# Index dot products of two query tiles in another order, selection rounds paced two and then three a unit, and one scaling moved from VectorE to ScalarE

## The chip, the cores and the metric

One core of a Trainium2 chip runs the whole kernel. The metric is device time in microseconds (us), the median of several executions. TensorE (PE, with its weight loads PEld) multiplies, VectorE (DVE), ScalarE (ACT) and GpSimd (POOL) work on vectors, SyncE (SP) issues most DMAs. Each engine runs its instructions in the order in which they were put into its queue.

## The reference

One decoder layer on 512 tokens and 16 prepended meta tokens (528 positions, width 1024): half-step SwiGLU FFN, a mixer, half-step SwiGLU FFN. The mixer has four heads of differential attention ("kind 0") and four heads of indexer-selected sparse attention ("kind 1"). For the second kind an indexer scores every key for every query, and only the top 128 keys of a query are attended to:

```python
u = rmsnorm(h, mix_norm) @ w_in
qa, ka, va, qb, ckv, iq, ik, iw = split(u)
# per block of 128 queries
dots = einsum('bqhd,bkd->bqhk', iq, ik)                  # 8 index heads of 64
score = einsum('bqh,bqhk->bqk', iw * 8 ** -0.5, relu(dots * 64 ** -0.5))
_, sel = top_k(where(causal, score, -inf), min(128, stop))
q_lat = rmsnorm(einsum('blhd,hdc->blhc', qb, b_w_uk))    # 4 heads, 256 wide
s = einsum('bqhc,bqkc->bhqk', q_lat, c[sel]) * 256 ** -0.5 + bias
```

## The kernel before

The program is one straight line of instructions without loops at run time. FFN 1 and FFN 2 (roughly the first 350 us and the last 340 us) are not touched. Matrix products are made in two parts, high and low: ACT writes the rounded high part, DVE subtracts to get the low part, and TensorE does three products (high by high, high by low, low by high).

The mixer has two stages.

**Projection stage** (about 380 to 475 us). A key projection `ik` and four index query projections `iq0` to `iq3` (line 1040, 24 matmuls of 512 columns each; `iq` c holds index heads 2c and 2c+1) come first, then three projections by `natural` (line 916). `pe_q` (line 873) is a list of small pieces of work, one per query tile t and index head hd: `dots_unit(t, hd)` (line 942) does two matmuls (line 949), a ReLU on ACT (line 951) and a multiply-add into the score of the tile on DVE (lines 954 and 957). `fill(1)` takes one piece off the list: `iq2` and `iq3` call it after each of their eight weight chunks, `natural` after each tile and half (12 matmuls). Tiles 0 to 3 have 144, 272, 400 and 528 keys. After the last head of tile 0 a small step drops its lowest keys (line 977). After the last head of tile 1, sixteen selection rounds and a mask go into DVE's queue at lower priority (line 962). A round (line 988) finds the eight largest scores and strikes them out, two passes over the tile's scores. For tiles 2 and 3 sixteen rounds and a mask each are appended to the list `selects` instead: 34 entries, used later.

**Attention stage** (about 475 to 670 us). 32 units, in the order of line 1139: kind 0 heads 0, 1, 2, kind 1 head 0, kind 0 head 3, kind 1 heads 1, 2, 3, each with query tiles 0 to 3. So units 0 to 11 are of kind 0, units 12 to 15 are the first of kind 1, and 16 to 19 are of kind 0 again. Step i of the loop (line 1465) holds the softmax of unit i (`u_soft`, line 1244, whose bias-add and minimum on DVE is line 1253), the normalisation of unit i-1, transposes and splits of unit i-2, `select(3)`, and the scores of unit i+1. `select(k)` (line 1238) takes k entries off `selects` and puts them behind the DVE work of the step, at slightly lower priority. A unit of kind 1 and tile t adds the mask of its tile on POOL (`u_mask`, line 1208, called one step ahead), so tile 2's mask is needed by unit 14 and tile 3's by unit 15. Other projections run as filler between units. `q_latent(hd)` (line 1373) makes the query of a kind 1 head in pieces, one per step: three products per tile, evacuation with a scale on ACT (line 1383), sums of squares on ACT (line 1389), a reciprocal root, four multiplications of a 128x256 tile by a column on DVE (line 1394), then transposes (line 1399) and their split (lines 1401, 1402).

The order on each engine is not the order of the text alone: a scheduler places instructions by priority when it expects their inputs, so a piece may slide past others.

Of the kernel before, what the change touches and what calls it, by code (L numbers as in the profile page):

```python
# [14 lines left out]
AF = mybir.ActivationFunctionType  # L15
# [38 lines left out]
def f32(ap):  # L54
    return ap.bitcast(F32)
# [145 lines left out]
def layer(ctx: ExitStack, tc: tile.TileContext, xT, gcols, kvg, lamv, rel, onehot,  # L201
# [4 lines left out]
    PE, V, A, G = nc.tensor, nc.vector, nc.scalar, nc.gpsimd  # L206
# [12 lines left out]
    def pa(name):  # L219
        return cur[0].tile([P, 2, 512], F32, tag="pa", bufs=3, name=name)  # L220
# [79 lines left out]
    def rsqrt_start(o, ss, n):  # L300

        A.activation(o, ss, AF.Ln, scale=1.0 / n, bias=epst)
        A.activation(o, o, AF.Exp, scale=-0.5)
# [576 lines left out]
    def proj_t(ps, full, nfill=0, w=None):  # L880
        wh, wl = w or ws.get()
        wh = wh[:, :1024].rearrange("p (k m) -> p k m", k=KC)
        wl = wl[:, :1024].rearrange("p (k m) -> p k m", k=KC)
        cols = [(0, T // 2), (T // 2, T)] if full else [(META, T)]
        for k in range(KC):
            for p_, (w, x) in enumerate(((wh, hgh), (wh, hgl), (wl, hgh))):
                for i, (a, b) in enumerate(cols):
                    o = ps[:, i, : b - a] if full else ps[:, : b - a]
                    PE.matmul(o, w[:, k, :], x[:, k, a:b], start=(k == 0 and p_ == 0),  # L889
                              stop=(k == KC - 1 and p_ == 2))  # L890
            if nfill and k % nfill == nfill - 1:
                fill(1)
# [49 lines left out]
    def dots_unit(t, hd):  # L942
        c, b = hd // 2, 64 * (hd % 2)
        K = kts(t)
        parts = [(0, K)] if K <= 512 else [(0, K // 2), (K // 2, K)]
        for (u0, u1) in parts:
            ps = dot_bank()[:, : u1 - u0]
            for p_, r in enumerate((ikh, ikl)):
                PE.matmul(ps, (iqh, iql)[hd % 2][c][:, t * P: (t + 1) * P], r[:, u0:u1], start=(p_ == 0), stop=(p_ == 1))
            rl = tmp[hd % 2][:, u0:u1]  # L950
            A.activation(rl, ps, AF.Relu, scale=I_D ** -0.5)
            sc = scores[t][:, u0:u1]
            if hd == 0:
                V.scalar_tensor_tensor(sc, rl, wq[:, t, hd: hd + 1], bias_win(cau, t)[:, u0:u1],
                                       op0=OP.mult, op1=OP.add if t == 0 else OP.subtract)
            else:
                V.scalar_tensor_tensor(sc, rl, wq[:, t, hd: hd + 1], sc, op0=OP.mult, op1=OP.add)
        if hd == I_H - 1 and t >= 2:
            selects.extend([lambda: topk_round(t)] * (TOPK // 8))
            selects.append(lambda: topk_mask(t))  # L960
        elif hd == I_H - 1:
            with tc.high_priority(offset=-1000):
                if t == 0:
                    drop_lowest()
                else:
                    for r in range(TOPK // 8):
                        topk_round(t)
                    topk_mask(t)
# [47 lines left out]
    def queue_dots(ts, hds):  # L1016
        for t in ts:
            for hd in hds:
                pe_q.append(lambda t=t, hd=hd: dots_unit(t, hd))
# [20 lines left out]
    for c in range(4):  # L1040
        ps = pa(f"iq{c}")[:, 0, :]
        proj_t(ps, False, 1 if c > 1 else 0)

        for q, r, o in ((iqh[c], 0, 64), (iql[c], 64, 0)):
            A.activation(q[r: r + 64], ps[r: r + 64], AF.Copy)
            V.tensor_sub(q[o: o + 64], ps[r: r + 64], f32(q[r: r + 64]))
        if c == 1:
            queue_dots((0, 1), range(4))
    queue_dots((0, 1), range(4, 8))
    queue_dots((2, 3), range(8))  # L1050

    def ckv_finish():
# [79 lines left out]
    def bank(tag):  # L1132
        return pp2.tile([P, 512], F32, tag=tag, bufs=nbank[tag], name=f"p_{tag}")
# [104 lines left out]
    def select(k):  # L1238

        with tc.issue_after(last[0].ins), tc.high_priority(offset=-100):  # L1240
            for _ in range(min(k, len(selects))):
                selects.pop(0)()
# [130 lines left out]
    def q_latent(hd):  # L1373
        ukh, ukl = uku
        qlraw = buf["ql"][:, :1024].rearrange("p (t c) -> p t c", t=NQ)
        ss = small.tile([P, NQ], F32, tag="qss", name="qss")
        for t in range(NQ):
            if t % 2 == 0:
                pq = bank("ch").rearrange("p (b c) -> p b c", b=2)
            for p_, (l, r) in enumerate(((qbh, ukh), (qbh, ukl), (qbl, ukh))):  # L1380
                PE.matmul(pq[:, t % 2, :], l[hd][:, t * P: (t + 1) * P], r[:, hd, :],
                          start=(p_ == 0), stop=(p_ == 2))
            A.activation(qlraw[:, t, :], pq[:, t % 2, :], AF.Copy, scale=Rn[:, t + 1: t + 2])
        qdone.add(hd)
        yield
        y = small.tile([P, NQ], F32, tag="rqy", bufs=2, name="rqy")
        w = small.tile([P, NQ], F32, tag="rqw", bufs=2, name="rqw")
        for t in range(NQ):
            A.activation(qll[hd][:, 0, :DC], qlraw[:, t, :], AF.Square, accum_out=ss[:, t: t + 1])
        rsqrt_start(y, ss, DC)  # L1390
        yield
        rsqrt_refine(y, ss, DC, w)
        for t in range(NQ):
            V.tensor_scalar_mul(qlraw[:, t, :], qlraw[:, t, :], y[:, t: t + 1])
        yield
        for c in range(2):
            pt = bank("ch")
            for t in range(NQ):
                PE.transpose(pt[:, t * P: (t + 1) * P], qlraw[:, t, c * P: (c + 1) * P], ident)
            g = gb[:, c: c + 1]  # L1400
            A.activation(qlh[hd][:, c, :], pt, AF.Copy, scale=g)
            V.scalar_tensor_tensor(qll[hd][:, c, :], pt, g, f32(qlh[hd][:, c, :]),
                                   op0=OP.mult, op1=OP.subtract)
            if c == 0:
                yield
        qready.add(hd)
# [39 lines left out]
    def advance(gs_, k=99):  # L1446
        for g in list(gs_)[:k]:
            if next(g, 1) == 1:
                gs_.remove(g)
# [14 lines left out]
    i = 0  # L1464
    while i < n or chains or qchains or st:
        if 0 <= i - 1 < n:
            u_norm(i - 1)
        advance(chains)
        if 0 <= i - 2 < n:
            u_trans(i - 2)  # L1470
        if i < n:
            u_soft(i)
        advance(qchains, 1)
        if 0 <= i - 2 < n:
            u_high(i - 2)
        advance(chains)
        if 0 <= i - 2 < n:
            u_low(i - 2)
        select(3)
        if i + 1 < n:  # L1480
            u_mask(i + 1)
            score_step(i + 1)
        if 0 <= i - 2 < n and units[i - 2][2] == NQ - 1:
            kind, hd, t = units[i - 2]
            b = bsel[(i - 2) // 4]
            G.tensor_copy(aM[b][32: 32 + META, :], f32(aM[b][:META, :]))
            chains.append((head_a, head_b)[kind](hd, b))
            next(chains[-1])
        if i == QS:
            fill_to(99)  # L1490
            uku += [w[:, :1024].rearrange("p (h c) -> p h c", h=B_H) for w in ws.get(ahead=False)]
            for x in ("ql", "vv", "sq"):
                buf[x] = wpool.tile([P, WSLOT], F32, tag="raw", bufs=3, name=f"buf_{x}")
            wo_load(0)
            stage += [buf["sq"][:, x * SEQ: (x + 1) * SEQ] for x in range(2)]
            late_load(0)
            late_conv(0)
        if QS < i <= QS + 6:
            x = i - QS - 1
            if x % 2 == 0:  # L1500
                q_b(1 + x // 2, lw)
            else:
                late_conv((x + 1) // 2)
            if x == 5:
                uvu += [w[:, :1024].rearrange("p (h c d) -> p h c d", h=B_H, c=2) for w in lw]
                clear(aM[1])
        for hd in range(A_H):
            if i == max(QS + 2 * hd, units.index((0, hd, NQ - 1))):
                qchains.append(q_latent(hd))
        fill_to(fill_at[i] if i < len(fill_at) else 99)  # L1510
        if all(h in adone for h in range(KA)):
            ready += 0.8
        while wo_done <= KC and (wo_done < int(ready) or i == n - 1):
            wo_step(wo_done)
            wo_done += 1
        if i == n - 1:
            ws.limit = n_plain2
            ws.conv(V)
        i += 1
# [109 lines left out]
```

## Time and profile before

| | us |
|---|---|
| median of 3 runs | 1044.72 |
| lowest, highest | 1044.2, 1045.92 |
| the profiled execution | 1045.36 |
| its span, first to last instruction | 1043.6 |
| PE busy in the span | 1017.4 (97%) |
| DVE busy | 847.3 (81%) |
| ACT busy | 567.5 (54%) |
| POOL busy | 31.9 (3%) |

Times within the span count from its first instruction. A busy PE is a modelled time: matmuls overlap in it, and it can hide small gaps. An idle time of an engine has a releaser, the instruction that the next one waited for. The chain of waits is followed back from the last instruction.

### The profile page before, as it was taken

How to read it: one execution, taken by the hardware profiler on the slowest of the kernel's cores; microseconds unless marked ns; L12 is line 12 of the kernel's file. 1: busy time of each engine (PE TensorE's matmuls, PEld its weight loads, DVE VectorE, ACT ScalarE, POOL GpSimd, SP SyncE). 2: the span in 40 equal slices, each digit the busy share in tenths (PEclk: the TensorE clock that was granted, in tenths of full speed). 3: DMA queues.
4: the chain of work that ended last, by engine and by line, in shares of the span. 5: the costliest groups of instructions: out<-in, count | busy, mean ns of one | idle time of the engine just before them, and what ended most of it. 6: DMA issues, size and time to landing. Idle time of an engine off the chain costs nothing.

```text
span 1043.6 us, 19433 instructions
## 1 busy us (share of the span) xinstructions
PE 1017.4 (97%) x7569; PEld 958.6 (92%) x7569; DVE 847.3 (81%) x1632; ACT 567.5 (54%) x1125; POOL 31.9 (3%) x51
## 2 busy tenths in 40 slices
PE   7999999999999999999998999999999999999998
PEld 7999999999999997998886788788899999999998
DVE  7968988889876756699899878487889999997754
ACT  7535656566243454565665786455457666653322
POOL 0000000000000000000010222000000000000000
PEclk9999999999999999999999999999999999999999
DMA  6263222324264332220201115462422333243640
GB/s 226 94 214 106 101 102 102 103 87 138 77 219 133 99 114 81 79 67 28 92 31 31 59 49 168 136 200 86 153 86 102 122 103 121 82 134 101 193 119 21
DMA packets 42440, 113.80 MB, mean 109 GB/s; under 512 B 5314, under 2 KB 8642, under 8 KB 42348
## 3 DMA queue, kind: packets, MB, share of 16 engines
q1 hardware_dynamic: 40268, 106.79, 31.5%
q0 software_dynamic: 1792, 5.48, 1.6%
q8 instruction: 59, 0.97, 0.4%
q10 hardware_dynamic: 288, 0.29, 0.1%
q14 instruction: 33, 0.27, 0.1%
HBM read 104.06 MB, written 11.50 MB: 111 GB/s over the span
## 4 chain that ended last, share of the span: by engine, by line
PE 88%; DVE 7%; ACT 2%; issue 1%; DMA 1%; POOL 0%; ACTq 0%; DVEq 0%; POOLq 0%
PE X L193 17%; PE Z L682 11%; PE V L193 8%; PE X L695 7%; PE g L435 6%; PE u L435 6%; PE nat L933 5%; PE Y L193 4%; PE V L695 3%; PE p_ch L1156 3%; PE wo L1416 3%; PE p_ch L1309 2%; PE iq L889 2%; PE Y L695 2%; PE p_ch L889 2%
## 5 line engine op out<-in xcount | busy, mean ns | idle before, releaser
L193 PE MATMUL X<-AR,ws 128*128 128x264 f32 (+1 forms) x1224 | 158.7, 281 | 0.3
L193 PEld LDWEIGHTS X<-AR,ws 128*128 128x128 f32 x1224 | 150.4, 188 | 1.1 <-ACT FA L501 0.9
L174 ACT ACTIVATE ws<-h 128x512 fp32r<-128x512 f32 x120 | 75.2, 628 | 40.6 <-PE V L193 14.4
L175 DVE TENSOR_TENSOR ws<-h,ws 128x512 fp32r<-128x512 f32 x120 | 82.2, 687 | 13.4 <-ACT ws L174 12.5
L101 ACT ACTIVATE wh<-wr 128x1024 fp32r<-128x1024 f32 (+3 forms) x54 | 53.7, 996 | 57.3 <-issue 12.1
L193 PE MATMUL V<-AR,ws 128*128 128x264 f32 (+1 forms) x624 | 82.2, 281 | 0.0
L102 DVE TENSOR_TENSOR wl<-wr,wh 128x1024 fp32r<-128x1024 f32 (+3 forms) x54 | 61.6, 1143 | 20.8 <-ACT wh L101 20.7
L193 PEld LDWEIGHTS V<-AR,ws 128*128 128x128 f32 x624 | 77.3, 188 | 0.1
L435 PE MATMUL g<-hg,wh 128*128 128x264 f32 (+1 forms) x288 | 63.8, 330 | 6.8 <-ACT hg L325 6.8
L435 PE MATMUL u<-hg,wh 128*128 128x264 f32 (+1 forms) x288 | 61.4, 321 | 0.0
L933 PE MATMUL nat<-wh,hg 128*128 128x256 f32 (+1 forms) x304 | 58.0, 285 | 0.0
L435 PEld LDWEIGHTS g<-hg,wh 128*128 128x128 f32 x288 | 46.6, 196 | 11.2 <-ACT hg L325 6.8
L682 PE MATMUL Z<-AR,wd 128*128 128x264 f32 (+1 forms) x432 | 55.1, 283 | 0.0
L682 PEld LDWEIGHTS Z<-AR,wd 128*128 128x128 f32 x432 | 53.1, 188 | 0.4 <-DVE FA L509 0.2
L435 PEld LDWEIGHTS u<-hg,wh 128*128 128x128 f32 x288 | 44.8, 189 | 4.7 <-ACT wh L101 0.6
L650 ACT ACTIVATE wd<-h 128x768 fp32r<-128x768 f32 (+1 forms) x28 | 23.0, 823 | 46.5 <-PE Z L682 19.6
L933 PEld LDWEIGHTS nat<-wh,hg 128*128 128x128 f32 x304 | 47.7, 188 | 0.3
L175 DVE TENSOR_TENSOR ws<-wr,ws 128x512 fp32r<-128x512 f32 x58 | 39.6, 685 | 8.1 <-ACT ws L174 7.8
L174 ACT ACTIVATE ws<-wr 128x512 fp32r<-128x512 f32 x58 | 36.3, 626 | 17.7 <-PE Y L193 5.5
L650 ACT ACTIVATE wd<-wd 128x768 fp32r<-128x768 f32 (+1 forms) x30 | 24.2, 808 | 36.3 <-PE Z L682 10.2
L1156 PE MATMUL p_ch<-wh,hg 128*128 128x256 f32 x224 | 42.4, 286 | 0.3 <-ACT wh L101 0.3
L933 PE MATMUL nat<-wl,hg 128*128 128x256 f32 (+1 forms) x152 | 42.7, 282 | 0.0
(389 smaller groups left out, 2627.6 us busy)
## 6 DMA issues: line engine op xcount, KB each, us to landing
wr<-w1u SPq DMA_DIRECT2D x17, 512.0 KB, 3.2
wr<-w2u SPq DMA_DIRECT2D x17, 512.0 KB, 3.2
wr<-w2g SPq DMA_DIRECT2D x15, 512.0 KB, 3.3
wr<-w1g SPq DMA_DIRECT2D x14, 512.0 KB, 3.3
wr<-win_n SPq DMA_DIRECT2D x12, 512.0 KB, 3.3
h<-w1g SPq DMA_DIRECT2D x7, 512.0 KB, 3.2
h<-w2g SPq DMA_DIRECT2D x7, 512.0 KB, 3.3
h<-w1d SPq DMA_DIRECT2D x8, 384.0 KB, 3.2
```

Of the source, the lines that this page charges most:

```text
L101: self.nc.scalar.activation(hi[:, c], r[:, c], AF.Copy)
L102: (low or self.low).tensor_sub(lo[:, c], r[:, c], f32(hi[:, c]))
L174: self.nc.scalar.activation(hi, x, AF.Copy)
L175: V.tensor_sub(lo, x, f32(hi))
L193: self.nc.tensor.matmul(ps, l[:, w], self.rhs(q, r, k), start=(p in FIRST and k == 0 and x == 0), stop=(k == KC // 2 - 1 and x == 2), skip ...
L435: PE.matmul(ps[:, i, : b - a], w[:, k, :], x(kk)[:, a:b], start=(kk == 0 and p_ == 0), stop=(kk == ktot - 1 and p_ == 2))
L650: A.activation(hi, x, AF.Copy)
L682: PE.matmul(dps["Z"][b], l[:, k * P: (k + 1) * P], u[f][:, o: o + hn], start=(f == 0 and x == 0), stop=(f == NDN - 1 and x == 2))
L695: PE.matmul(ps, w[:, k * P: (k + 1) * P], sub_(u, k, k + 1)[:, 0], start=(p in FIRST and k == 0 and x == 0), stop=(k == KS - 1 and x == 2) ...
L889: PE.matmul(o, w[:, k, :], x[:, k, a:b], start=(k == 0 and p_ == 0), stop=(k == KC - 1 and p_ == 2))
L933: PE.matmul(ps, xx[:, kk, a:b], w[:, k, :], start=(kk == 0 and p_ == 0), stop=(kk == KC - 1 and p_ == 2))
L1156: PE.matmul(ps, xx[:, kk, a:b], w[:, kk % 4, :], start=(kk == 0 and p_ == 0), stop=(kk == KC - 1 and p_ == 2))
```

## The change

Three edits. First, the dot products of tile 1 are queued ahead of those of tile 0, and the heads of `iq2` and `iq3` are queued as soon as these are there: 8 pieces after `iq1`, 4 after `iq2`, 4 after `iq3`. Before it was 8 after `iq1` and 8 after `iq3`, so no piece was left for `iq3`'s calls of `fill`. Tiles 2 and 3 follow as before. Second, `select` takes two entries a step up to step 7 and three from step 8. Before, three a step, the 34 entries were used up at step 11; now they last until step 13. Third, the four multiplications of `q_latent` are done by ACT (copy with a scale column) and no longer by DVE.

```diff
@@ projection stage
-        if c == 1:
-            queue_dots((0, 1), range(4))
-    queue_dots((0, 1), range(4, 8))
+        if c > 0:
+            queue_dots((1, 0), range(2 * c if c > 1 else 0, 2 * c + 2))
     queue_dots((2, 3), range(8))
@@ q_latent
         for t in range(NQ):
-            V.tensor_scalar_mul(qlraw[:, t, :], qlraw[:, t, :], y[:, t: t + 1])
+            A.activation(qlraw[:, t, :], qlraw[:, t, :], AF.Copy, scale=y[:, t: t + 1])
@@ loop over units
-        select(3)
+        select(2 if i < 8 else 3)
```

## Rows read from the trace of the kernel before

**Rows 1.** The page: shares of the chain that ended last, by engine.
```profile
PE 88%; DVE 7%; ACT 2%; issue 1%; DMA 1%; POOL 0%; ACTq 0%; DVEq 0%; POOLq 0%
```
**Rows 2.** Busy by stretch: length, busy PE, PEld, DVE, ACT, POOL, clock, DMA.
```profile
404.00:424.00 20.00, 19.16 (x107) 16.04 (x106) 11.60 (x19) 9.72 (x19) 0.00 (x0) 1.00 0.24 79
424.00:440.00 16.00, 15.88 (x129) 15.25 (x128) 10.95 (x31) 9.20 (x23) 0.00 (x0) 1.00 0.15 57
440.00:475.00 35.00, 34.61 (x273) 33.20 (x272) 33.84 (x86) 21.12 (x52) 0.93 (x2) 1.00 0.20 69
475.00:481.00 6.00, 3.84 (x33) 3.29 (x32) 5.79 (x19) 2.12 (x5) 0.00 (x0) 1.00 0.27 90
481.00:544.00 63.00, 62.06 (x467) 55.50 (x467) 59.46 (x169) 38.10 (x98) 2.57 (x4) 1.00 0.12 40
544.00:590.00 46.00, 41.38 (x238) 33.03 (x238) 43.64 (x129) 30.99 (x89) 7.68 (x10) 1.00 0.20 63
...
596.00:604.00 8.00, 8.00 (x32) 6.49 (x32) 5.09 (x18) 5.21 (x15) 0.60 (x1) 0.57 0.01 2
604.00:667.00 63.00, 60.70 (x368) 51.65 (x367) 45.24 (x132) 42.96 (x124) 13.61 (x16) 1.00 0.43 130
```
**Rows 3.** PE's waits in 404 to 440: line and releaser, us, times, longest.
```profile
PE dt L949 <- DVE AR L1046: 0.8, 2, 0.5
```
**Rows 4.** PE's waits in 440 to 481.
```profile
PE p_s L1226 <- DVE mn L1253: 1.5, 1, 1.5
PE p_ch L1156 <- DVE wl L102: 0.7, 1, 0.7
```
**Rows 5.** The chain of waits from 472 to 482: start, us, what.
```profile
475.83 1.22 DVE wl L102
...
478.91 0.46 DVE m L990
...
479.39 0.52 DVE FA L991 x2
```
**Rows 6.** DVE in order of time, 424 to 500: first, then late tile 1 rounds.
```profile
438.35 0.44 DVE L990 MAX8 m<-FA 128x8 f32<-128x272 f32 x1
...
471.83 0.43 DVE L990 MAX8 m<-FA 128x8 f32<-128x272 f32 x1
```
**Rows 7.** PE's waits in 481 to 544.
```profile
PE p_ch L1156 <- DVE wl L102: 0.5, 2, 0.3
```
**Rows 8.** The chain of waits from 544 to 560: one round of tile 3.
```profile
550.31 0.62 DVE m L990
...
551.00 0.74 DVE FA L991 x2
```
**Rows 9.** DVE in order of time: unit 8's softmax, tile 3's fifth round.
```profile
544.13 0.28 DVE L1253 CUSTOM_DVE_ANT_0 fa<-p_s,FA 128x144 f32<-128x144 f32 x1
...
548.06 0.70 DVE L990 MAX8 m<-FA 128x8 f32<-128x528 f32 x1
```
**Rows 10.** DVE and POOL, 579 to 590: unit 13, mask, its use, unit 15.
```profile
580.22 0.42 DVE L1253 CUSTOM_DVE_ANT_0 fa<-p_s,fa 128x272 f32<-128x272 f32 x1
581.92 0.52 DVE L994 TENSOR_SCALAR FA<-FA 128x528 f32<-128x528 f32 x1
582.52 1.35 POOL L1211 TENSOR_TENSOR fa<-FA 128x528 f32<-128x528 f32 x1 [0.37 <-DVE FA L994]
584.77 0.65 POOL L1486 CAST AR<-AR 16x512 fp32r<-16x512 f32 x1
588.68 0.40 DVE L1253 CUSTOM_DVE_ANT_0 fa<-p_s,fa 128x264 f32<-128x264 f32 x1
```
**Rows 11.** DVE in order of time: the four scalings of one head.
```profile
610.45 1.14 DVE L1394 TENSOR_SCALAR buf_ql<-buf_ql,rqy 128x256 f32<-128x256 f32 x4
```
**Rows 12.** ACT in order of time: two copies with a scale column, same shape.
```profile
543.54 0.81 ACT L1383 ACTIVATE buf_ql<-p_ch,Rn 128x256 f32<-128x256 f32 x2
```
**Rows 13.** The chain of waits from 624 to 635, around a head's scalings.
```profile
629.56 0.61 DVE buf_ql L1394 x2
```

## The prediction

> **What bounds the kernel now.** I read the chain of waits first: PE carries most of it, DVE a small part [rows 1]. So the question for any edit on DVE or ACT is where PE stands still because of them. The busy times by stretch answer that [rows 2]. PE's length minus its busy time is 0.84 us in 404 to 424, 0.12 in 424 to 440, 0.39 in 440 to 475, 2.16 in 475 to 481, 0.94 in 481 to 544, 4.62 in 544 to 590 and 2.30 in 604 to 667: 11.4 us in all. That is about what the mixer can give back (a busy PE hides small gaps, so somewhat more). DVE in the same rows is busy 11.60 of 20 and 10.95 of 16 us up to 440, then 33.84 of 35, 5.79 of 6, 59.46 of 63 and 43.64 of 46. So DVE has slack before 440 and hardly any from 440 to 590, while PE has none to speak of before 475. From 596 to 604 the granted clock is 0.57, mostly the lower of the two levels.
>
> **The profiled execution.** It took 1045.36 us for a span of 1043.6, and lies 0.64 above the median of 1044.72. The terms below are differences; I apply them to 1045.36 and take off the 0.64.
>
> **Edit 1, what it moves.** Nothing is added or removed: 32 pieces of dot products stay 32. Four pieces (heads 4 and 5 of tiles 1 and 0) go from the first `natural` into `iq3`, which had none, so every later piece comes four fills earlier. Tile 1's last head moves from the eighth fill after `iq3` to the second, and with it the start of its sixteen rounds. No DMA moves in program order; SP's loads wait for buffers as before, and POOL's only related load, of a bias row, waits for tile 3's first piece and comes earlier too. Tile 0's last head stays the fourth fill, so the small step behind it stays.
>
> **Edit 1, the gain.** Two waits end in 475 to 481: PE waits 1.5 us for unit 0's softmax on DVE and 0.7 for a weight split [rows 4]. The chain shows why: the split stands at 475.83, and between it and the softmax stand rounds of tile 1, each 0.46 + 0.52 with short issue times, about 1.0 [rows 5]. The first of these rounds is at 438.35 and six run from 471.83 on (their first is shown) [rows 6]. DVE was idle 16 - 10.95 = 5.05 us in 424 to 440 [rows 2], where rounds can now run: up to five of them, more than the two and a half that the chain shows behind the split. I take 2.1 of the 2.16. Bounds: 0 (the scheduler spends the slack otherwise) and 2.5 (with part of 440 to 475).
>
> **Edit 1, the cost.** PE waits 0.8 us in `iq2` for DVE to split `iq1`, just before the pieces of heads 2 and 3, which need it [rows 3]. Now `iq3` meets heads 4 and 5 just behind the split of `iq2`, and the first `natural` meets heads 6 and 7 at once behind that of `iq3`. Behind the waiting piece on PE stand the other matmuls of the projection. One more such wait is 0.8, two are 1.6; none at all if the scheduler lets pieces slide. I take 0.8, since `natural` has 12 matmuls between fills to hide the second. Bounds 0 and 1.6.
>
> **Edit 2, units 0 to 7.** Up to step 7 two entries a step take 16 instead of 24: a mask and seven rounds of tile 3 leave. A round of tile 3 is 0.62 + 0.74 = 1.36 us on the chain [rows 8]. But the queue was late: tile 3's fifth round, queued at step 7, runs only at 548.06, behind unit 8's softmax at 544.13 [rows 9]. So in time only four rounds and a mask leave the stretch before 544: 4 x 1.36 + 0.4 = 5.8 us (0.4 for tile 2's mask: the 0.52 of tile 3's [rows 10] by 400 of 528 keys). DVE has that much less of 59.46 [rows 2]. PE stood still 0.94 us there, over half of it for weight splits on DVE [rows 2, 7]. I take 0.9. Bounds 0 and 1.5 (gaps that busy PE hides). The rest of the 5.8 buys nothing: PE is the bound there.
>
> **Edits 2 and 3, units 8 to 15.** The same 5.8 us come on top of 43.64 in 544 to 590. Edit 3 takes four scalings off DVE for each of two heads there, 1.14 a head by the nearest row [rows 11], 2.3 in all. That leaves 3.5 more; DVE was idle 46 - 43.64 = 2.36 [rows 2]. If all of that is filled, the stretch grows by 1.1. But units 8 and 9 also lose the late rounds ahead of them, which stood on the chain [rows 8]; I take 0.8. Bounds -1.5 (a third of the 4.62 of PE's idle time goes with the scalings) and +6.3 (below). What is late next is tile 3's mask: it ends near 582.4, POOL takes 1.35 to use it, and unit 15's softmax begins at 588.68, so 588.68 - 583.87 = 4.8 us of slack cover a later mask [rows 10]. Behind the waiting POOL instruction stand a bias load and a copy (at 584.77) that the head's last value product needs.
>
> **Edit 3, the last two heads.** One of these has scalings on the chain, 0.61 for two of them, with other DVE work of the chain behind them [rows 13]; DVE loses 1.14 there and the chain about 1.2. On ACT four copies cost 4 x 0.4 = 1.6, by two of the same shape in 0.81 [rows 12], against 1.14 [rows 11]; ACT is busy 42.96 of 63 [rows 2], which mostly hides it. For the other head I give back 0.3, most of the 1.6 - 1.14 = 0.46 by which its query comes later. Together 0.9 gained. Bounds 1.5 gained and 2.0 lost (four heads, each 0.46 later).
>
> **The sum.** -2.1 + 0.8 - 0.9 + 0.8 - 0.9 = -2.3. 1045.36 - 2.3 = 1043.1 for an execution like the profiled one, and 1043.1 - 0.64 = 1042.4 against the median.
>
> **Rivals.**
> *The late mask (slower).* Before, rounds ran up to two units after they were queued [rows 9]. If at step 13 the queue is still one unit behind, six entries stand behind unit 13's softmax at 580.22: 5 x 1.36 + 0.52 = 7.3. The other DVE work up to unit 15 is the 8.5 from 580.22 to 588.68, less a round's rest and the mask (0.74 + 0.52) and less one head's scalings (1.14): 6.1. So the mask ends near 593.6, POOL's use of it at 595.0, and unit 15 begins 6.3 late [rows 8, 10, 11]. It decides from the point at which the mask is over 4.8 late. In place of +0.8 it puts +6.3: 1042.4 + 5.5 = 1047.9. For it: DVE is already full there. Against: fewer rounds before 544 let the queue catch up.
>
> *PE was the bound anyway (no change).* Only half of the 2.16 goes, both waits on splits come, and the 0.9 in units 0 to 7 was not the rounds' doing: -1.0 + 1.6 - 0.4 + 0.8 - 0.9 = +0.1, so 1044.8.
>
> *Scaling late on ACT (no change).* If ACT's queue makes the query later, the 0.9 gained becomes 2.0 lost: 1042.4 + 2.9 = 1045.3. The nearest row has 0.4 against 0.29 a tile [rows 11, 12]. The Trainium skill speaks for this rival: "ScalarE: Activation LUTs", in its rules for kernel authors, sends multiplications to VectorE and not to ScalarE. By that rule the edit is a loss and the time 1045.3, by the rows of idle ACT 1042.4; the trace agrees on the price of one tile and leaves open whether anyone waits.
>
> *The clock stays up (faster).* From 596 to 604 PE's clock was 0.57 of full [rows 2]; work of 8 x 0.57 = 4.6 us at full speed took 8. If units 12 to 17 fall otherwise and it doesn't drop, up to 3.4 more comes back: 1039.0.
>
> **How the numbers follow.** The forecast has 0.42, late mask 0.20, PE bound anyway 0.16, late on ACT 0.07, clock 0.15. About 0.2%, or 2.1 us, is what a measurement of this kernel can tell from no change, so faster lies under 1042.6 and slower over 1046.8. The forecast's own range is 1040 to 1044; I put 0.32 of its 0.42 under 1042.6. Faster: 0.32 + 0.15 = 0.47. Same: 0.10 + 0.16 + 0.06 = 0.32. Slower: 0.20 + 0.01 = 0.21. The range for 8 in 10 reaches from 1038.2 (into the clock case) to 1047.0, and leaves out most of the late mask's far side.
>
> **What would show it.** Right: the waits of PE on unit 0's softmax and on the split near 476 are gone, tile 1's rounds begin near 424 and end before the attention stage; PE's waits on the index splits are about 1.6; the stretch from unit 0's to unit 8's softmax is shorter by 1 us, with DVE idle in it; the one from unit 8 to unit 16 is longer by 1 or less, and POOL's use of tile 3's mask ends before unit 15's turn. Wrong: PE waits on unit 15's softmax or POOL near 590, or on the scalings on ACT, or the low clock lasts longer or falls elsewhere.

## The result, and the profile after

The changed kernel took 1054.36 us (median of four runs), the kernel before 1044.61 in the same comparison: a ratio of 1.0097, with a 95% interval of 1.008 to 1.0114. So it is 9.75 us slower, where 2.3 us faster was forecast, and it lies outside the range. The profiled execution took 1054.49 us for a span of 1052.7, at a mean granted clock of 0.990 against 0.997.

The slower rival of the prediction, the late mask, is what the trace shows, at nearly twice its price (12.3 us from unit 8 to unit 15, where it had 6.3). First the busy time by stretch (columns as in [rows 2]; the stretch from 590 is put here in place of 596 to 604):

```profile
404.00:424.00 20.00, 19.35 (x105) 15.67 (x104) 12.29 (x21) 10.40 (x22) 0.00 (x0) 1.00 0.19 62
424.00:440.00 16.00, 15.23 (x118) 14.30 (x117) 14.73 (x41) 8.73 (x22) 0.00 (x0) 1.00 0.16 57
...
475.00:481.00 6.00, 4.52 (x37) 3.81 (x36) 3.51 (x12) 2.69 (x9) 0.00 (x0) 1.00 0.29 87
481.00:544.00 63.00, 62.26 (x470) 56.02 (x469) 52.85 (x154) 38.43 (x99) 2.57 (x4) 1.00 0.15 50
544.00:590.00 46.00, 42.48 (x234) 33.48 (x232) 43.16 (x121) 34.06 (x99) 4.60 (x7) 0.96 0.16 51
590.00:604.00 14.00, 7.11 (x32) 6.02 (x33) 10.51 (x37) 5.00 (x16) 3.09 (x4) 0.50 0.07 20
604.00:667.00 63.00, 60.68 (x370) 51.98 (x370) 42.49 (x123) 47.12 (x134) 14.27 (x16) 0.98 0.31 96
```

Up to 590 little is lost: PE stands still 1.48 us in 475 to 481, not 2.16, VectorE has 10 us of idle time in 481 to 544, not 3.5, and unit 14 starts 1.5 us earlier than before. Then come 14 us in which PE is busy for half the time, at 0.50 of its clock, which is the lower of the two levels, 1.2 GHz. Before, PE was busy all of 590 to 604 at a mean clock of 0.76:

```profile
590.00:604.00 14.00, 14.00 (x73) 10.73 (x72) 10.09 (x38) 10.80 (x34) 1.38 (x2) 0.76 0.06 16
```

The waits of PE of the changed kernel from 590 to 612 (line and releaser, us, times, longest) point at the cause:

```profile
PE p_s L1225 <- DVE mn L1252: 4.2, 1, 4.2
PE p_ch L1332 <- DVE ray L309: 2.4, 1, 2.4
```

Lines beyond 1049 are one lower than before, so L1252 is the softmax, L1210 the GpSimd addition of bias and mask, L994 the mask, L1398 and L1393 the latent transposes and scalings. VectorE, GpSimd and PE in order of time (start, us, engine, operation, idle time before it and who ended it):

```profile
597.17 0.43 DVE L994 TENSOR_SCALAR FA<-FA 128x528 f32<-128x528 f32 x1
...
597.74 1.33 POOL L1210 TENSOR_TENSOR fa<-FA 128x528 f32<-128x528 f32 x1 [15.50 <-DVE FA L994]
...
599.11 0.43 DVE L1252 CUSTOM_DVE_ANT_0 fa<-p_s,fa 128x264 f32<-128x264 f32 x1 [1.51 <-POOL fa L1210]
...
599.60 2.02 PE L1225 MATMUL p_s<-AR 64*128 64x144 f32 x10 [4.18 <-DVE mn L1252]
```

The mask of the fourth query tile (tile 3) ends at 597.6, not at 582.4 [rows 10]. GpSimd, idle for 15.5 us, waits for it, unit 15's softmax waits for GpSimd, and PE for the softmax. That is the chain which the rival had named. Followed back from there, the chain of waits stays on VectorE among the rounds of tile 3 for some 14 us (start, us, what):

```profile
583.88 0.71 DVE m L990
...
595.89 0.70 DVE FA L991
...
597.25 0.36 DVE FA L994
...
597.74 1.34 POOL fa L1210
```

PE's other wait, 2.4 us for `ray`, comes of the same rounds: `ray` takes three short steps on VectorE (588.68, 590.82 and 591.90), and passes of rounds stand between them.

The starts of some units' softmaxes on VectorE, in us from the start of each span, for this kernel and for runs told of below (e1: edits 1 and 3; e2: edit 2; e4: edit 3; e6: edits 1 and 3 without the second latent head; e14: half of edit 2):

| unit | before | after | e1 | e2 | e4 | e6 | e14 |
|---|---|---|---|---|---|---|---|
| 0 | 480.5 | 479.4 | 479.3 | 480.8 | 480.0 | 479.5 | 479.3 |
| 8 | 544.1 | 542.2 | 542.9 | 545.0 | 545.1 | 543.1 | 543.7 |
| 14 | 586.0 | 584.5 | 585.3 | 586.5 | 585.9 | 584.0 | 588.8 |
| 15 | 588.7 | 599.1 | 586.5 | 602.0 | 587.2 | 586.6 | 595.0 |
| 19 | 601.3 | 613.3 | 602.9 | 618.2 | 604.6 | 598.2 | 615.1 |
| 24 | 627.6 | 634.4 | 629.9 | 640.0 | 631.9 | 622.2 | 637.5 |
| 31 | 660.2 | 667.3 | 664.1 | 672.1 | 664.6 | 655.2 | 669.6 |
| span | 1043.6 | 1052.7 | 1047.0 | 1055.0 | 1048.5 | 1038.1 | 1052.7 |

From unit 8 to unit 15 the changed kernel needs 56.9 us and the one before 44.6. The mask alone doesn't explain the table, though: e4 loses nothing at unit 15 and is 3.3 us late at unit 19. That is the clock.

**How clock and stalls are told apart below.** Each run has its mean granted clock beside its time. Of the 100 executions of the kernel before that ran beside the experiments, those at 1.000 took 1042.3 us on average (11), those at 0.997 1044.9 (20), those at 0.993 1048.0 (6). A straight line through all 100 gives 1042.0 us at full clock and 0.88 us for each 0.001 below it (correlation 0.92). For every kernel I give the mean clock and the *time at full clock*, its mean time less 0.88 per 0.001. This is an estimate: a clock that is low while PE stands still costs less, so it takes off too much there.

| run | what it has | median us | ratio to before, 95% interval | mean clock | at full clock |
|---|---|---|---|---|---|
| before | | 1044.6 | | 0.997 | 1042.0 |
| after | all three edits | 1054.36 | 1.0097 (1.008 to 1.0114) | 0.9908 | 1046.8 |
| e1 | edits 1, 3 | 1049.04 | 1.004 (1.0027 to 1.0054) | 0.9915 | 1041.5 |
| e2 | edit 2 | 1056.37 | 1.0107 (1.0092 to 1.0121) | 0.9872 | 1044.7 |
| e3 | edit 1 | 1044.99 | 0.9998 (0.9985 to 1.0011) | 0.9961 | 1041.5 |
| e4 | edit 3 | 1049.30 | 1.0047 (1.0034 to 1.0059) | 0.9902 | 1041.0 |
| e5 | all, unit 15 free | 1053.20 | 1.0075 (1.0051 to 1.0099) | 0.9875 | 1042.3 |
| e6 | 1, 3 but second head | 1041.40 | 0.9979 (0.9958 to 1.0) | 0.9972 | 1039.7 |
| e7 | 3, second head alone | 1048.14 | 1.0036 (1.002 to 1.0053) | 0.9944 | 1043.6 |
| e8 | edit 2, then four a unit | 1052.97 | 1.0073 (1.0049 to 1.0098) | 0.9900 | 1044.3 |
| e9 | all but second head | 1058.63 | 1.0137 (1.0115 to 1.016) | 0.9858 | 1046.8 |
| e10 | e9, unit 15 free | 1053.40 | 1.0076 (1.0057 to 1.0096) | 0.9882 | 1042.7 |
| e11 | e1, 12 fill matmuls | 1048.84 | 1.0037 (1.0022 to 1.0052) | 0.9952 | 1044.4 |
| e12 | 1, 3 for heads 2 and 3 | 1044.70 | 1.0001 (0.9987 to 1.0014) | 0.9956 | 1041.0 |
| e13 | e10, 20 fill matmuls | 1058.63 | 1.0136 (1.0111 to 1.0161) | 0.9890 | 1049.1 |
| e14 | half of edit 2 | 1054.09 | 1.0084 (1.0062 to 1.0106) | 0.9878 | 1042.9 |
| e15 | e6, 4 fill matmuls | 1042.83 | 0.9993 (0.9975 to 1.001) | 0.9974 | 1041.6 |
| e16 | e6, four a unit in front | 1057.44 | 1.011 (1.0078 to 1.0142) | 0.9858 | 1043.6 |
| e17 | e10, six rounds fewer | 1048.45 | 1.0016 (0.9997 to 1.0035) | 0.9917 | 1040.4 |
| e18 | e6 once more | 1044.35 | 0.9983 (0.9966 to 1.0) | 0.9958 | 1040.4 |

One of the eleven executions of e3, at 2772 us, is left out of its mean. By this fit, of the result's mean loss of 10.1 us about 4.8 are there at full clock and about 5.3 are clock (0.997 to 0.9908).

The profiled executions allow a second estimate, which doesn't take off too much where PE stands still: PE's idle time in the span, and what the clock cost, that is PE's busy time by one less the granted clock, summed over stretches of 1 us.

| us | before | after | e1 | e2 | e4 | e5 | e6 | e9 | e10 | e14 | e17 |
|---|---|---|---|---|---|---|---|---|---|---|---|
| PE idle | 26.2 | 33.2 | 25.0 | 32.9 | 26.1 | 27.5 | 24.2 | 34.7 | 27.8 | 26.9 | 25.2 |
| clock | 3.4 | 6.7 | 10.2 | 9.6 | 10.2 | 12.4 | 0.0 | 9.4 | 12.1 | 12.7 | 8.5 |
| the rest | 1014.0 | 1012.7 | 1011.8 | 1012.5 | 1012.3 | 1012.0 | 1013.9 | 1012.1 | 1012.0 | 1013.1 | 1012.3 |

The rest of the span is the same within some 2 us in all of them, so the two upper rows hold nearly all of the differences. In this execution the change lost 7.0 us by waits (2.1 of them at the output projection, see e7) and 3.3 by the clock, so the clock's share lies between a third and a half.

### The profile page after: what moved, and what is told of

Same layout as the page of the kernel before. It is cut to its first block, busy times and chain, and to the rows that moved or that the text cites. A ratio compares the mean times of both kernels' runs of the same rounds, so it can differ in the third digit from the quotient of the medians.

```text
span 1052.7 us, 19424 instructions
## 1 busy us (share of the span) xinstructions
PE 1019.5 (97%) x7569; PEld 960.2 (91%) x7569; DVE 843.1 (80%) x1616; ACT 573.9 (55%) x1141; POOL 31.8 (3%) x51
## 4 chain that ended last, share of the span: by engine, by line
PE 88%; DVE 6%; ACT 4%; issue 1%; DMA 1%; POOL 0%; ACTq 0%; DVEq 0%; POOLq 0%
PE X L193 17%; PE Z L682 11%; PE V L193 9%; PE X L695 7%; PE g L435 6%; PE u L435 6%; PE nat L933 4%; PE Y L193 4%; PE p_ch L1155 3%; PE V L695 3%; PE wo L1415 3%; PE p_ch L889 2%; PE iq L889 2%; PE p_ch L1308 2%; PE Y L695 2%; PE p_ch L1415 1%
## 5 line engine op out<-in xcount | busy, mean ns | idle before, releaser
L175 DVE TENSOR_TENSOR ws<-h,ws 128x512 fp32r<-128x512 f32 x120 | 82.1, 686 | 13.4 <-ACT ws L174 12.7
L101 ACT ACTIVATE wh<-wr 128x1024 fp32r<-128x1024 f32 (+3 forms) x54 | 53.6, 995 | 59.3 <-issue 12.1
L650 ACT ACTIVATE wd<-wd 128x768 fp32r<-128x768 f32 (+1 forms) x30 | 24.2, 808 | 36.6 <-PE Z L682 10.2
```

Of the source, the lines that this page charges most:

```text
L101: self.nc.scalar.activation(hi[:, c], r[:, c], AF.Copy)
L175: V.tensor_sub(lo, x, f32(hi))
L650: A.activation(hi, x, AF.Copy)
```

## The experiments

### The edits one by one (e1 to e4)

Edit 2 alone (e2) is one line of the kernel before:

```diff
-        select(3)
+        select(2 if i < 8 else 3)
```

> Edit 2 alone: two rounds a unit up to unit 7, then three. Theory: seven rounds of the fourth query tile fall behind unit 8, its mask comes 15 us late, the GpSimd addition of unit 15 waits for it: 1054 to 1058 us, the softmax of unit 15 near 600. Rival (it takes the ScalarE scaling or the new order to make the mask late): under 1048 us.

It took 1056.37, as the theory said, and unit 15 starts at 602.0. GpSimd waits for the mask in it too:

```profile
600.45 1.47 POOL L1211 TENSOR_TENSOR fa<-FA 128x528 f32<-128x528 f32 x1 [18.00 <-DVE FA L994]
```

So edit 2 makes the mask late without help from the others. The other two edits together (e1) are the diff of the change without that line:

> Edits 1 and 3 without edit 2: three rounds a unit all through. Theory (the moved rounds are what costs): the softmax of unit 15 starts near 588 as before, not at 599, and the gain of the order and of the scaling stays: 1041 to 1043.5 us, by the sum's -2.1 + 0.8 - 0.9 = -2.2. Rival (the scaling on ScalarE or the new order costs the 10 us): 1047 us or more, with the late start of unit 15 still there.

It took 1049.04: a miss for the theory, at the rival's price but without the rival's sign, since unit 15 starts at 586.5, earlier than before. Edit 1 (e3) and edit 3 (e4) alone tell which of them it is:

> Edit 1 alone. Theory: the sum's -2.1 + 0.8, so 1043.0 to 1044.0 us, unit 0's softmax about 1 us earlier and tile 1's selection rounds some 12 us earlier. Rival (TensorE was the bound there anyway): within 0.3 us of before, at no change of where unit 8 starts. If the order made the mask late: over 1046 us.

> Edit 3 alone. Theory: -0.9 for the last two heads and no loss at units 8 to 15: 1043.3 to 1044.3 us. Rival (a scaling queued on ScalarE behind the exponentials comes late): 1045.3 us, and TensorE then waits on the scaling's split at the heads of units 8 to 15.

Edit 1 is no measurable change, 1044.99, and a gain of some 0.5 us at full clock. Edit 3 alone costs 4.9 by the ratio, 1049.30, though at full clock it gains about 1. Its loss is all clock, by the second estimate too (26.1 us of idle time as against 26.2, and 10.2 of clock as against 3.4). PE and ScalarE near 588 in e4, in order of time:

```profile
587.15 1.29 ACT L1394 ACTIVATE buf_ql<-buf_ql,rqy 128x256 f32<-128x256 f32 x3
588.35 0.58 ACT L1319 ACTIVATE buf_vv<-p_ch 128x512 f32<-128x512 f32 x1
...
588.98 1.05 PE L1324 MATMUL p_ch<-onesr,buf_vv 128*128 128x1 f32 x8 [0.75 <-ACT buf_vv L1319]
```

and PE in the kernel before:

```profile
588.49 1.05 PE L1324 MATMUL p_ch<-onesr,buf_vv 128*128 128x1 f32 x8 [0.20 <-ACT buf_vv L1319]
```

Three scalings of the second latent head (head 1) stand on ScalarE ahead of the square that PE needs next, which comes 0.51 later, and PE waits 0.75 instead of 0.20. That is not the 4.9; but from 590.0 on the clock is at its lower level, up to 607, where before it was from 596.0 to 603.5. The stretch from 587 to 604 in e4 and in the kernel before (busy time as above):

```profile
587.00:597.00 10.00, 9.25 (x49) 6.91 (x47) 5.28 (x26) 7.45 (x23) 1.25 (x2) 0.65 0.16 51
597.00:604.00 7.00, 7.00 (x28) 5.58 (x29) 3.53 (x8) 3.64 (x12) 0.60 (x1) 0.50 0.01 2
```

```profile
587.00:597.00 10.00, 9.80 (x67) 7.42 (x66) 8.88 (x34) 8.63 (x28) 1.26 (x2) 0.97 0.17 56
597.00:604.00 7.00, 7.00 (x28) 5.70 (x28) 4.13 (x14) 4.34 (x14) 0.60 (x1) 0.55 0.01 2
```

In the first ten microseconds PE issues 49 matmul records instead of 67, though it is shown busy for nearly as long. A new theory, then: those three instructions, through PE's small wait, bring the low clock forward by 6 us.

### The second latent head (e6, e18, e7, e12)

e6 is e1 with the second head back on VectorE; e12 leaves the first there too (`hd < 2`), and e7 is the kernel before with that head alone on ScalarE (`hd != 1`):

```diff
-            A.activation(qlraw[:, t, :], qlraw[:, t, :], AF.Copy, scale=y[:, t: t + 1])
+            if hd == 1:
+                V.tensor_scalar_mul(qlraw[:, t, :], qlraw[:, t, :], y[:, t: t + 1])
+            else:
+                A.activation(qlraw[:, t, :], qlraw[:, t, :], AF.Copy, scale=y[:, t: t + 1])
```

> Edits 1 and 3, but the second latent head (the one scaled near 587 us) is scaled on VectorE as before; three rounds a unit. Theory: on ScalarE three of that head's scalings stood ahead of the square of head 1's values (buf_vv), TensorE waited 0.75 instead of 0.20 us there, and the low clock began near 590 instead of 596 and lasted twice as long. Without them the low stretch is near 7 us again: 1043 to 1045.5 us. Rival (the scaling costs in all heads, or the low clock's length is chance): 1048 us or more, as edits 1 and 3 took 1049.0.

1041.40, better than the theory asked for: a ratio of 0.9979 where e1 has 1.004. At full clock it is 2.1 under the kernel before, about what the sum without edit 2 had forecast. Its profiled execution (1038.1) had no low clock at all in the mixer. Run again beside the kernel before:

> Edits 1 and 3 with the second head on VectorE, beside the kernel before on this chip: 1040.5 to 1043 us, 1.5 to 3 us under the kernel before, from a clock near 0.997 as before and 2 us less of waits. If the earlier 1041.4 was luck with the clock: within 1 us of before.

1044.35 against 1045.58: outside the range, and 1.2 under the kernel before, where chance with the clock was to give 1 at most. At full clock it is again 2.0 less. The clock of this kernel scatters from 0.990 to 1.000, and both intervals touch 1.0. So the medians of both comparisons and the time at full clock speak for a gain of some 2 us, but the measured times alone don't show it.

> Only the second latent head's four scalings moved to ScalarE, nothing else changed. Theory (these four make TensorE wait on the square near 588 and bring the low clock early): 1048 to 1050 us, with a low stretch of 14 us or more from 590 on. Rival (all heads cost): under 1046 us.

1048.14, the time of the theory, but its profile is not: PE waits 0.76 at the square, yet the clock was low only from 597.5 to 605, and twice before (365.5 to 369.5, 481.5 to 485.5). The mean clock of 12 runs, 0.9944 against 0.9973, is worth 2.6. The other 1.7 at full clock has a cause of its own: a wait of PE for `AR` at the output projection, 2.1 us, which four kernels have (after, e7, e9, e13) and the others don't. In the changed kernel's waits from 667 to 700 it is

```profile
PE wo L1415 <- DVE AR L1369: 2.1, 1, 2.1
```

So e1 against e6 and e7 show that the second head's scalings cost clock on average. That the longer wait at the square is what does it isn't shown: e7 has that wait without the early fall.

> Edit 1, and edit 3 for the last two latent heads alone; three rounds a unit. Theory (the gain of edit 3 lies at the last two heads and its loss at the second): as with only the second head on VectorE, 1040.5 to 1043 us. Rival (the first head's scaling on ScalarE matters too): outside of that, by 1 us or more against 1041.4.

1044.70. At full clock it gains 0.7, e6 2.1 (2.0 in e18): so most of edit 3's good seems to come from the first head, which the prediction had put among units 8 to 15. From unit 10 to unit 12 the kernel before takes 18.1 us, e12 18.1 and e6 17.1.

### The changed kernel with one thing taken away (e9, e5, e10, e17)

e9 is the whole change with the second head on VectorE. e5 is the whole change with unit 15's addition freed of the mask, e10 has both ("the kernel before this one" in its text is e9):

```diff
-            G.tensor_add(TB[i % 2][:, : kts(t)], bias_of(i), scores[t])
+            G.tensor_add(TB[i % 2][:, : kts(t)], bias_of(i), bias_of(i) if i == 15 else scores[t])
```

> The whole change, but the second latent head is scaled on VectorE as before, so this is edit 2 on top of the kernel of 1041.4 us. Theory (the mask is late whatever the scaling does, and TensorE's stall by it brings the low clock of itself): 1051 to 1055 us. Rival (the low clock of the changed kernel comes from the second head's scaling, as in edits 1 and 3): 1044 to 1048 us.

> The whole change, with unit 15's GpSimd addition reading its bias twice instead of the bias and the selection mask: it leaves the mask out of unit 15's scores, all rounds and the mask itself still run. Theory (the price of edit 2 is the wait of unit 15 for the mask): no wait of TensorE of over 1 us on unit 15's softmax, and what stays is edits 1 and 3, which took 1049.0 us: 1047 to 1050 us. Rival (the moved rounds cost on VectorE itself, whoever waits for the mask): 1052 us or more.

> The kernel before this one, with unit 15's GpSimd addition reading its bias twice: it leaves the selection mask out of unit 15's scores. Neither the wait for the mask nor the second head's scalings on ScalarE are in it. Theory (those two are the whole loss): 1041 to 1044 us. Rival (the moved rounds on VectorE keep the low clock long, as with unit 15 free and the scaling in, 1053.2): 1049 us or more.

All three speak against "the wait plus the second head". e9 took 1058.63, more than its theory and its rival allowed; e5, at 1053.20, and e10, at 1053.40, are at the time of their rivals, in which the moved rounds cost on VectorE whoever waits for the mask. By the ratios taking the wait away gave back 2.3 us (the change to e5) and 6.4 (e9 to e10), of which 2.1 are the wait at the output projection, which the two with the wait happen to have. The traces show why it is so little: PE's idle time falls by 5.7 and 6.9 us, and the clock's cost rises by 5.7 and 2.7. Against the kernel before, e10 has 1.6 us more of idle time and 8.7 more of clock. Its stretch at the low level is 590.0 to 611.0:

```profile
590.00:611.00 21.00, 17.84 (x61) 13.05 (x62) 15.04 (x51) 12.72 (x38) 1.38 (x2) 0.51 0.00 1
```

And e9 is slower than the change by 4.2 us by the ratios: its scalings of the second head stand on VectorE at 585.82 for 1.13 us, ahead of the mask, and unit 15 starts 1.7 later. So in the company of edit 2 the scalings on ScalarE help; the rest of the 4.2 isn't traced. The same four instructions are a loss in e4 and a gain between e9 and the change.

Why is it low for so long in e10? Tile 3's rounds stand on VectorE up to 599.5 in it, between the softmaxes and ahead of other work: PE waits 1.4 us for `ray` there, with passes of rounds before and between its steps. Unit 16's starts at 595.9, unit 17's at 601.0 and unit 18's at 608.9 (before: 590.0, 593.1, 596.7). e17 takes the last six of these rounds away:

```diff
-            selects.extend([lambda: topk_round(t)] * (TOPK // 8))
+            selects.extend([lambda: topk_round(t)] * (10 if t == 3 else TOPK // 8))
```

> The whole change without the second head's scaling on ScalarE and without unit 15's wait (1053.4 us), and with ten rounds on the fourth query tile instead of sixteen: it leaves out the last six rounds of that tile's selection, 8 us of VectorE work between 586 and 600, and the mask of unit 15's scores. Theory (those late rounds between the softmaxes starve TensorE, and the clock falls and stays low): the low stretch is 8 us at most, the softmaxes of units 16 to 18 come as in the kernel of 1041.4 us, and the time is 1040 to 1043 us. Rival (the bunching at units 8 to 13 or something else takes the clock): 1048 us or more.

1048.45, in the rival's range: the late rounds aren't all of it. Units 15 to 18 start at 585.4 to 595.9, within 1.3 us of e6, and PE's waits near there are those of e6 or shorter (0.70 and 0.20 us). And yet the clock fell at 587.5 and stayed low to 605. The same matmuls at either level, first e6, then e17 (PE in order of time):

```profile
585.33 0.44 PE L1308 MATMUL p_ch<-AR 80*128 80x512 f32 x1
586.46 1.05 PE L1323 MATMUL p_ch<-onesr,buf_vv 128*128 128x1 f32 x8 [0.20 <-ACT buf_vv L1318]
591.11 1.15 PE L1338 MATMUL p_ch<-buf_vv,ident 4*128 4x128 f32 x8
596.54 0.50 PE L1308 MATMUL p_ch<-hg,AR 128*128 128x512 f32 x1
```

```profile
584.01 0.45 PE L1308 MATMUL p_ch<-AR 80*128 80x512 f32 x1
585.14 1.05 PE L1323 MATMUL p_ch<-onesr,buf_vv 128*128 128x1 f32 x8 [0.20 <-ACT buf_vv L1318]
591.57 2.07 PE L1338 MATMUL p_ch<-buf_vv,ident 4*128 4x128 f32 x8
599.91 0.80 PE L1308 MATMUL p_ch<-hg,AR 128*128 128x512 f32 x1
```

Between the value products of one head (up to 585.8 in e6) and those of the next (from 596.5) PE has only small work: 1-column sums, transposes of 128 columns, 64-row scores, 4-row broadcasts, products of 256 columns. In e6 that stretch passed at 2.4 GHz in 10.7 us. In e17 the clock falls 3 us after its beginning, the rest of the stretch runs at 1.2 GHz, 15.5 us in all, and the clock comes back only after the wide products of the next head are running. So late rounds lengthen the stretch, and taking six away gave back about 6 us by the ratios (1.0076 and 1.0016); but what tips the clock near its beginning isn't settled by e17.

### The dose (e14, e8, e16)

> Half the dose of edit 2 on the kernel before: two rounds a unit up to unit 3 only, so three or four rounds move behind unit 8 instead of seven. Theory (the price has a threshold: the mask must be there when unit 15's addition asks for it, near 582.5, with under 5 us of slack): the mask comes near 588 to 591 and the time is 1046 to 1051 us. Rival (the price goes with the number of rounds moved): 1050 to 1051 us, half of edit 2's 11.5. Rival (under the threshold): within 1.5 us of before.

With `2 if i < 4 else 3` the mask comes at 593.0, later than expected, and unit 15 at 595.0, 6.3 us late: the 593.6 and 6.3 of the prediction's rival, though that had worked them out for the full dose. The time, 1054.09, is beyond what the theory and either rival allowed. GpSimd's addition (it names a reciprocal that ended with the mask) and the stretches of this run:

```profile
593.61 1.33 POOL L1211 TENSOR_TENSOR fa<-FA 128x528 f32<-128x528 f32 x1 [8.39 <-DVE rs L1268]
```

```profile
544.00:590.00 46.00, 42.27 (x230) 33.55 (x229) 43.30 (x124) 29.50 (x88) 4.58 (x7) 0.96 0.14 47
590.00:611.00 21.00, 18.94 (x67) 13.67 (x68) 13.18 (x50) 10.71 (x33) 3.68 (x5) 0.52 0.13 40
```

By the ratios half the dose costs 8.8 us and the full dose (e2) 11.2, so the price doesn't go with the rounds moved. A threshold fits, though only two doses were run, and in e14 the clock is most of the bill: 21 us at 0.52, and by the second estimate 9.3 us of clock and 0.7 of idle time more than before.

> Edit 2 with four rounds a unit from unit 8 on instead of three. Theory A (the rounds are late since a unit lets only three go): the mask comes one to two units earlier than in edit 2 alone, before unit 15 asks for it: 1045 to 1049 us. Theory B (VectorE, busy 43.6 of the 46 us from 544 to 590, has no room for seven more rounds of 1.36 us): the softmaxes of units 11 to 14 come later by what the mask comes earlier, 1052 us or more.

With four a unit from unit 8 on: 1052.97, theory B's time but not its reason. GpSimd adds at 595.07, 5.4 earlier than in e2, and the units before didn't get later for it (unit 14 at 586.9, e2 586.5). But unit 15, at 596.8, is still 8.1 us later than before, and the clock is low from 589.0 to 606.5. One round a unit more was too little to catch up in six units.

> Edits 1 and 3 with the second head on VectorE and the pacing turned the other way: four rounds a unit up to unit 7, then three. Theory (VectorE's room near 585 to 600 is what counts, the front has cover): the mask comes near 570 and the time is 1039.5 to 1042.5 us. Rival (VectorE, 95% busy from 481 to 544, has no room in front): 1044 us or more, the loss in units 0 to 7.

With `4 if i < 8 else 3` on e6 the mask is there at 569.7, and the time is 1057.44: the rival was right about the sign, but not about the place. From unit 0 to unit 8 it loses 1.9 against e6 (65.5 us against 63.6); then unit 11 is at 568.1, 11.0 later than in e6, among rounds that now follow each other every 2 us from 550 to 569, and the clock is low from 559.5 to 570.5 and again from 597.5 to 615. So three a unit stands between two losses, in these runs.

### Holding the clock with wide work (e11, e13, e15)

```diff
         advance(qchains, 1)
+        if i in (14, 15, 16):
+            fill = bank("ch")
+            for _ in range(4):
+                PE.matmul(fill, uku[0][:, 0, :P], cth[:, 0, :512], start=True, stop=True)
```

> Edits 1 and 3 (1049.0 us, of it 8.9 at the low clock) with twelve 512-column matmuls more, four in each of the steps of units 14, 15 and 16, into a PSUM bank that nobody reads. At full clock they cost 12 x 0.23 = 2.8 us at most. Theory (TensorE's thin work between 584 and 604, stalls and small matmuls, is what takes the clock down): the low stretch shrinks, 1042 to 1046 us. Rival (the low clock comes of itself): 1050 to 1053 us.

The theory holds for the clock and fails for the sum: 1048.84 is in neither range. On e1, whose low stretch was 14 us, it is now 4 (589.5 to 593.5), and the mean clock rises from 0.9915 to 0.9952, worth 3.3. The stretches:

```profile
589.00:594.00 5.00, 5.00 (x26) 3.78 (x25) 1.04 (x8) 3.81 (x11) 0.21 (x1) 0.66 0.13 39
594.00:604.00 10.00, 10.00 (x59) 7.54 (x59) 7.51 (x25) 7.54 (x26) 0.60 (x1) 1.00 0.01 2
```

The first and the second group of four, in PE's order of time:

```profile
584.06 1.09 PE L1476 MATMUL p_ch<-AR,wh 128*128 128x512 f32 x4
...
591.14 2.05 PE L1476 MATMUL p_ch<-AR,wh 128*128 128x512 f32 x4
```

The second runs at the lower level, and right behind it the clock is back. But the twelve matmuls cost about 2.9 at full clock, and the time is no better than the 1049.04 of e1. So wide work at this place shortens the low stretch, and is no remedy.

> The whole change without the second head's scaling and without unit 15's wait (it leaves the selection mask out of unit 15's scores), which took 1053.4 us, of it 12.3 at the low clock; with twenty 512-column matmuls more, four in each of the steps of units 14 to 18, into a PSUM bank that nobody reads: 20 x 0.23 = 4.7 us at full clock. Theory (the moved rounds delay the softmaxes of units 16 to 18, and what that costs is the clock that falls while TensorE has thin work): 1045 to 1049 us, at a mean clock of 0.994 or more. Rival (the delay itself costs): 1054 us or more.

> Edits 1 and 3 with the second head on VectorE (1041.4 us, clock between 0.990 and 1.000) and four 512-column matmuls more in the step of unit 16. Theory (the clock that falls near 596 can be held by a little wide work): 0.9 us at most of added work against up to 3 us, 1040 to 1042 us with a clock of 0.998 or more in most runs. Rival (the four are too few, or at the wrong place): 1042 to 1044 us.

Twenty matmuls in e10 (e13) don't hold the clock: it is low from 591 to 612 as before, and the time is 1058.63. PE waits 2.4 us there at 592.5 for VectorE. Since the clock wasn't held, the run doesn't tell clock from delay. The second estimate does so in part: e10's later softmaxes left PE idle for only 1.6 us more than before. Four matmuls in e6 (e15) leave the mean clock as it was, 0.9974, and cost 1.5 us by the ratios; 1042.83 is in the rival's range.

## Why the prediction was wrong

**Where PE is bound.** Right for what could be gained: the gains showed where PE had stood still. The loss came from 590 to 604, where PE had been busy without a gap, and the low clock there was seen only as something that could go away.

**Edit 1.** The mechanism was right. Tile 1's first round moves from 438.35 [rows 6] to 426.11, the wait for unit 0's softmax falls from 1.5 [rows 4] to 0.8, and unit 0 starts 1.0 to 1.2 earlier in the change, e1 and e6 (e3's profiled execution starts it at 481.7, behind a low clock from 365.5 to 369.5). The size was off: PE's idle time in 475 to 481 shrank by 0.7, not 2.1, since half of the wait and all of the 0.7 for the weight split remain (the same in e6). The cost, +0.8, was smaller too: PE stands still 1.42 us in 404 to 440 and did 0.96 [rows 2]. The net of e3 at full clock is 0.5, not 1.3.

**Edit 2, units 0 to 7.** Right: forecast 0.9, measured 0.8. From unit 0 to unit 8 the change takes 62.8 us; e6, e1 and the kernel before take 63.6. (e2 takes 64.2, of which 1.7 are a low clock from 481.0 to 485.0.)

**Edits 2 and 3, units 8 to 15.** This is the step that failed. Forecast +0.8; the traces have +12.3 (56.9 us against 44.6 from unit 8 to unit 15), and e2 has +12.4. The sum counted DVE work against DVE's idle time in the stretch and let the rest fit. But a queue in order isn't a sum of work: before, a round already ran a unit behind the step that let it go [rows 9], the mask, let go at unit 11 (561.7), ran two units behind it [rows 10], and units 8 to 13 had next to no room to catch up, with VectorE busy for 43.64 of 46 us [rows 2]. In the changed kernel the mask, let go at unit 13 (575.6), runs at 597.2, behind unit 14. The argument against the rival, "fewer rounds before 544 let the queue catch up", fails by the trace: VectorE stood idle for 10 us in 481 to 544, and tile 3's first round, let go at unit 8 (542.2), ran at 548.3. The idle time came before these rounds were let go. Nor is unit 15's wait the whole loss: without it (e5, e10) the time stays at 1053, and unit 18 starts 11.6 and 12.2 us later than before, since the rounds then stand ahead of units 16 to 18.

**The rival late mask** had the chain right. Its times were too early: the mask ends at 597.6, not 593.6, unit 15 is 10.4 us late in the change and 13.3 in e2, and the 6.3 that it forecast is met by half the dose (e14), which is a coincidence. Its price was wrong too: "+6.3 late" was taken for 6.3 us of time. e14, with unit 15 6.3 late, lost 8.8, with 21 us at a clock of 0.52 in place of 7.5 us at the lower level; and e5 and e10 lost nearly as much without the wait. Both mistakes are in the upper bound and so in the range's upper end.

**Edit 3.** The last two heads gained 0.9 from unit 19 to unit 24 in e12 (25.4 us against 26.3), as forecast, and gave back 0.4 behind it. The rival "scaling late on ACT" came true at another place and by another consumer: not the query's split but the next square on ScalarE's queue, 0.55 us for PE. With it went a lower clock, and a loss of 4.9 in e4; how the one brings the other isn't shown. The prediction's price for it, 2.9 against the forecast, was half of what e4 shows (4.9 lost where 0.9 was to be gained), and it had a chance of 0.07. The rule of the Trainium skill ("ScalarE: Activation LUTs", rules for kernel authors), which sends multiplications to VectorE, would have kept the second head on VectorE and given up the first head's 1 us, which e6 has. The traces agree that VectorE is the faster (1.14 us for four scalings there [rows 11], 1.79 on ScalarE in e4). But the first head's gain came where VectorE was full, and the second head's loss where a square stood behind the scalings, so the rate doesn't decide it.

**The clock.** The prediction held that a stall costs its length; a longer low clock stood among its signs of being wrong, but had a price only as a possible gain. Between a third and a half of the loss is clock. The same kernel's mean clock differed from execution to execution (before: 0.993 to 1.000). The Trainium skill states something like it for a kernel's start ("TensorE: Matmul & The Clock Gate", Part 1): the same kernel shows different numbers of slow matmuls from run to run.

**What stays open.** Why the clock falls near the beginning of the small work in some executions and not in others, with the same waits (e6, e17); by what way the second head's scalings lower it (e7); and whether a held clock would give back what e5 and e10 lose, since no run held it there.

## What to carry to other kernels

Work that was let go in portions, in order, behind a busy engine didn't catch up, even in larger portions (e8): follow the queue to the first consumer of its last item, and to whatever else stands behind its items in the queue, and price a missed due time from the moment at which that consumer asks. Before moving an instruction to an idle engine, list what stands behind it there and who waits for that; four scalings gained 1 us in the first head, cost some 6 in the second (e1 against e6), and in that same head gained 4 beside another edit (the change against e9). A stretch of small matmuls on TensorE ran at half clock in some executions and at full clock in others, with the same waits ahead of it (e17, e6), so compare kernels at the granted clock of each run as well as by their times.

## What the runs showed of the hardware

The granted clock differed between executions of the same kernel, and most of the scatter in time follows it: 0.88 us per 0.001 in 100 executions of the kernel before. Low stretches fell at the same few places: near 365, 481, 546 to 560 and 635, mostly 3.5 to 4 us long, and near 590, up to 24.5 us long. While the clock was low there, PE could be shown busy without a gap (5.00 of 5 us at 0.66 in e11, 7.00 of 7 at 0.50 in e4), so the busy share hides it: the count of matmuls in a stretch and the clock column show it. Eight 4-row matmuls took 1.15 us at one level and 2.07 at the other. And with twelve matmuls more that nobody reads (e11) the low stretch was 4 us instead of 14, at no change of the time; twenty in e10 (e13) and four in e6 (e15) didn't raise the mean clock by more than 0.001.
